# Moving the opening loads of a hybrid decoder block: half a weight tile, the gate weights and the other constants

## The chip, the cores and the metric

The kernel runs on one core of a Trainium2 chip. The metric is the time of one execution in device microseconds (us). A core has five engines with an instruction queue each: TensorE (PE, matmuls; its weight loads are listed apart as PEld), VectorE (DVE), ScalarE (ACT), GpSimd (POOL) and SyncE (SP, which only issues DMAs). ScalarE and GpSimd can issue DMAs too; a DMA stands in the queue of the engine that issues it, and all queues are served by the core's 16 DMA engines. An engine works through its instructions in the order in which they were written for it: an instruction that waits holds up all that stand behind it.

## The reference

One decoder layer for 2048 tokens of width 1024, in float32. The input is normalised and projected once into the columns of two branches, which are mixed, gated, joined, projected out and added to the input; a last norm follows.

```python
n = rms_norm(h, norm_w[layer])
proj = jnp.einsum('bsd,de->bse', n, w_in[layer])
pu, pz, q, k, v, dz, b, a = [proj[..., int(offsets[i]):int(offsets[i + 1])] ...]
y_pool = pool_mixer(pu, pz, pool_w[layer], pool_scale[layer])
y_dn = deltanet_mixer(q, k, v, dz, b, a, conv_w[layer], a_log[layer], dt_bias[layer], dn_norm_w[layer])
y = jnp.concatenate([y_pool, y_dn], axis=-1)
h = h + jnp.einsum('bse,ed->bsd', y, w_out[layer])
...
return rms_norm(h, final_norm_w)
```

`pu` and `pz` (512 columns each) feed a causal pooling mixer with trailing windows of 2, 4, 8 and 16 tokens, `q`, `k`, `v`, `dz` (4 heads of 128 each) a gated delta rule in chunks with a short causal convolution, and `b`, `a` (4 columns each) are its gates, which the text calls the gate columns.

## The kernel before

**Tiling.** The tokens are taken in two blocks of 1024, each in two halves of 512. For the projection, tokens stand along the free axis: x is read transposed (`xT`), a tile of 128 input features by 512 tokens is one matmul step, and eight such steps (k = 0 to 7) sum one output tile of 128 columns in PSUM. Float32 is carried as two parts of the type float32r: a high part and the rest. `split_x` (L522) makes `nh` (ScalarE, L525) and `nl` (VectorE, L526) from an x tile, `split_w` (L713) makes `wh` (ScalarE, L716) and `wl` (VectorE, L717, recorded as L510) from a weight tile, and `project` (L722) issues three matmuls a step: `wh` with `nh` (L728), `wh` with `nl` (L729), `wl` with `nh` (L730). The norm's factor for each token is not applied to x; it is worked out from the rows of x beside the projection, and multiplied in when the sums are taken from PSUM.

**The opening.** The order of the first loads is as follows.

- ScalarE issues `norm_w`, both halves of the first weight tile (256 KB each, tile `qT`, L706) and the first constants `cst` (L1112).
- SyncE issues x of the first half in five pieces (L520; the first tile in two pieces, then tiles of two steps and 512 KB: two in tiles named `dec`, one `kdec`), the two halves of the second weight tile (L706), x of the second half (four tiles: `dec`, `kdec`, `kT`, `kT`), four row tiles of the first half (L533: `Ai`, `At`, `v`, `vT`, 512 KB each) and four of the second (`Tt`, `Tt`, `yr1`, `Ai`).
- `load_constants` (L475) then adds the gate weights `wba` (32 KB), two triangular matrices (`tri`, a tile named `X`, 128 KB), `dt_bias`, `a_log` (`nega`), the convolution's weights, `pool_w` (256 KB), `pool_scale` and the head norm's weight, all on SyncE.
- GpSimd issues the third weight tile (`wh`, 512 KB) at the start and adds its rest later (L720).

**What uses them.** Of each row tile ScalarE takes the sum of squares (L539); when the four of a half are done, `row_scale` (L541, GpSimd's L507), `row_diagonal` (L547, four VectorE scalings, L550) and a matmul against ones (`broadcast`, L554; L556) spread the norm's factors over the partitions (`rb`), and only then can that half's sums be taken from PSUM. The gate weights are split like the others: `whl` by a cast on ScalarE (L495) and a subtraction on VectorE (L496), both in `prepare_constants` (L494). The gate columns are a projection of their own (`gate_rows`, L560).

**What sets the order.** The program is traced as a list of events, each with a slot (`at`, L674). A `Planner` (L91) then writes the order of every engine anew: it knows a modelled cost for each instruction (L126), goes through modelled time, and lets each engine take the ready instruction that is due first, unless that would hold up one that is due sooner and ready soon (L306 to L321). Due times are worked backwards from PE's sequence in event order (L238 to L254). PE takes runs of matmuls in event order as far as they are ready, looking up to 24 runs ahead (L287). The DMAs traced before the mark `plan.opening` (L476) are taken in their traced order on their engine (L255, L308 to L314), and their landing is modelled as one pipe that all of them share (L387 to L389); other DMAs get a landing time of their own (L133 to L139). The planned order is bound (L396), so at run time nothing overtakes. A DMA of SyncE or ScalarE beyond the first eight also waits for an older one to land.

**Slots of the events concerned.** First weight tile -80, `cst` -79.5, x of the first half -79 to -76, second weight tile -72, x of the second half -71 to -68, rows -67 and -62, `load_constants` (and with it the opening mark) -45, `prepare_constants` -1.

Of the kernel before, what the change touches and what calls it, by code (L numbers as in the profile page):

```python
# [17 lines left out]
KT = D // P  # L18
# [41 lines left out]
E_PU, E_PZ, E_Q, E_K, E_V, E_Z = 0, 4, 8, 12, 16, 20  # L60
# [344 lines left out]
def hymba_kernel(  # L405
# [19 lines left out]
    nc = tc.nc  # L425
# [9 lines left out]
    plan = Planner(tc, nc.cur_bb.bb.instructions)  # L435

    def st(shape, dt, tag, bufs=1):
        return plan.tile(sp, shape, dt, tag, tag, bufs)


    def ct(shape, dt, name):
        return cp.tile(shape, dt, tag=name, name=name)
# [10 lines left out]
    wba = ct([P, KT, 8], F32, "wba")  # L453
# [19 lines left out]
            nc.tensor.matmul(ps[:, 0:P], ones, ones, start=True, stop=True)  # L473

    def load_constants():  # L475
        plan.opening = len(plan.traced)  # L476
        tri = st([P, 2, P], F32, "X")
        for dst, src in (
            (wba, w_ba),
            (tri, consts[:, C_LE:C_X0].rearrange("p (a b) -> p a b", a=2)),  # L480
            (dtb, dt_bias[None, :].to_broadcast([P, HEADS])),
            (nega, a_log[None, :].to_broadcast([P, HEADS])),
            (cw, conv_w),
            (pw, pool_w),
            (psc, pool_scale),
            (dnw, dn_w),
        ):
            nc.sync.dma_start(dst, src)
        nc.gpsimd.memset(halo_c, 0.0)
        nc.gpsimd.memset(halo_p, 0.0)  # L490
        nc.gpsimd.memset(state, 0.0)
        return tri
# [181 lines left out]
    def at(slot, fn, *args):  # L674
        events.append((slot, len(events), fn, args))
# [22 lines left out]
    def load_w(w, et, first):  # L698
        w["hi"] = st([P, KT, P], F32R, "wh", 3)
        w["lo"] = st([P, KT, P], F32R, "wl", 3)  # L700
        if first:
            w["raw"] = wr = st([P, KT, P], F32, *first)
            step = KT // 2
            eng = nc.scalar if et == E_PU else nc.sync
            for k in range(0, KT, step):
                eng.dma_start(wr[:, k : k + step], w_in[et, :, k : k + step])  # L706
        elif w["mixed"]:
            nc.gpsimd.dma_start(w["hi"], mixed[et - E_PU, 0])
            nc.gpsimd.dma_start(w["lo"], mixed[et - E_PU, 1])
        else:  # L710
            nc.gpsimd.dma_start(w["hi"], w_in[et])  # L711

    def split_w(w, et, first, part):  # L713
        if first:
            ks = slice(part * KT // 2, (part + 1) * KT // 2)
            nc.scalar.copy(w["hi"][:, ks], w["raw"][:, ks])  # L716
            split_lo(nc.vector, w["lo"][:, ks], w["raw"][:, ks], w["hi"][:, ks])  # L717
        elif not w["mixed"]:
            nc.scalar.activation(w["lo"], w["hi"].bitcast(F32), AF.Copy, scale=-1.0)  # L719
            nc.gpsimd.dma_start(w["lo"], w_in[et], accum_op=ALU.add)  # L720
# [31 lines left out]
    def gate(u, dst, rb):  # L752
        nc.vector.tensor_tensor(out=dst, in0=u["ps"], in1=rb, op=ALU.mult)
        nc.scalar.activation(dst, dst, AF.Silu)
# [355 lines left out]
    tri = []  # L1110
    at(-90, begin)
    at(-79.5, lambda: nc.scalar.dma_start(cst, consts[:, 0:C_TMP]))  # L1112
    at(-89, warm_up)
    at(-45, lambda: tri.append(load_constants()))
    at(-1, lambda: prepare_constants(tri[0]))
    for b in range(NB):
        n, gt = [None, None], {}
        units = []
        heads = [(h, {}) for h in range(HEADS)]
        pools = [(gi, {}) for gi in range(GROUPS)]  # L1120
        tiles = []
        for gi, res in pools[:lead]:
            tiles += [("pu", E_PU + gi, gi, res), ("pz", E_PZ + gi, gi, res)]
        for h, res in heads:
            kinds = (("k", E_K), ("q", E_Q), ("v", E_V), ("z", E_Z))
            tiles += [(kind, e0 + h, h, res) for kind, e0 in kinds]
        for gi, res in pools[lead:]:
            tiles += [("pu", E_PU + gi, gi, res), ("pz", E_PZ + gi, gi, res)]
        order = []
        i = 0  # L1130
        while i < len(tiles):
            if tiles[i][0] == "pu":
                order += [(tiles[i], 0), (tiles[i + 1], 0), (tiles[i], 1), (tiles[i + 1], 1)]
                i += 2
            else:
                order += [(tiles[i], 0), (tiles[i], 1)]
                i += 1
        for hf in range(NHALF):
            n[hf] = env = {}
            base = slot - (1 - hf) * 8 * PAIRED + 0.5  # L1140
            for i in range(KT // 2):
                at(base - L_X if b else -79 + 8 * hf + i, load_x, b, hf, i, env)
            for k in range(KT):
                at(base + 0.1 + k * (8 * PAIRED - 2) / KT, split_x, k, env)
            base += 8 * PAIRED - 2
            base += L_ROW if b else L_ROW0[hf]
            for j in range(NCH):
                at(base - L_XT + 4 * j if b else -67 + 5 * hf + 0.1 * j, load_rows, b, hf, j, env)
                at(base - L_XT + 8 + 4 * j if b else 4 + 8 * hf + j, square_rows, j, env)
            at(base - L_XT + 24 if b else base, row_scale, env)  # L1150
            at(base, row_diagonal, env)
            at(base + L_RB[b * NHALF + hf], broadcast, env)
            env["slot"] = base + L_RB[b * NHALF + hf] + 0.1
        for hf in range(NHALF):
            tg = slot + 8 * PAIRED * hf + (L_GR if b else L_GR0)
            at(tg, gate_rows, n, hf, gt)
            at(tg + L_GROW, gate_scale, n, hf, gt)
            at(tg + L_GROW + L_GCOL, gate_turn, hf, gt)
        ready = tg + L_GROW + L_GCOL + 0.1
        at(ready, gate_columns, gt)  # L1160
        ready += L_GATE
        at(ready, gate_sums, gt)
        ready += L_SUMS
        for h in range(HEADS):
            for hf in range(NHALF):
                at(ready + L_DEC * (2 * h + hf), decay, gt, h, hf)
        ready += L_DEC + 2
        ends = [dict() for _ in range(HEADS)]
        weights = {}
        for (kind, et, idx, res), hf in order:  # L1170
            if et not in weights:
                weights[et] = {"mixed": kind == "pu" and idx >= lead}
                first = ("qT", 2) if slot < 8 * PAIRED else None
                at(-80 + slot if first else slot - L_W, load_w, weights[et], et, first)
                at(slot - (16 if first else L_SPLIT), split_w, weights[et], et, first, 0)
                if first:
                    at(slot - 13, split_w, weights[et], et, first, 1)
            u = {"spare": 24 <= slot < 40}
            for k in range(KT):
                at(slot + k, lambda u=u, w=weights[et], n=n, hf=hf, k=k: project(u, w, n, hf, k))  # L1180
            slot += KT
            te = max(slot, n[hf]["slot"])
            if kind in "kqv":
                key = kind + "T"

                def evac(u=u, kind=kind, idx=idx, hf=hf, res=res, key=key, env=n[hf]):
                    if hf == 0:
                        res[key] = st([P, TB], F32, key, 1 if kind == "v" else 2)
                    conv_silu(u, "qkv".index(kind) * HEADS + idx, hf, res[key], env["rb"])

            elif kind == "z":

                def evac(u=u, hf=hf, res=res, env=n[hf]):
                    if hf == 0:
                        res["sz"] = st([P, TB], F32, "sz", 2)
                    gate(u, res["sz"][:, hf * HALF : (hf + 1) * HALF], env["rb"])

            elif kind == "pz":

                def evac(u=u, hf=hf, res=res, env=n[hf]):  # L1200
                    res["szp"] = st([P, HALF], F32, "szp", 1)
                    gate(u, res["szp"], env["rb"])

            else:

                def evac(u=u, b=b, idx=idx, hf=hf, env=n[hf]):
                    pool_mix(u, b, idx, hf, env["rb"])

                at(te + L_POOL, pool_out, u, b, idx, hf, res, weights[et]["mixed"])
            at(te, evac)  # L1210
            if kind in "kqvz":
                ends[idx][kind, hf] = slot
        for h, res in heads:
            delta(b, h, res, gt, ends[h], ready)
# [229 lines left out]
    for k in range(NP):  # L1444
        w = {}
# [110 lines left out]
```

## Time and profile before

| | |
|---|---|
| three runs | 934.34, 934.75, 937.35 us; median 934.75 |
| profiled execution | 933.28 us, of which the core's span 931.6 us |
| granted clock of TensorE, mean of the span | 0.991 |
| busy: PE, DVE, ACT, POOL | 909.4, 606.9, 475.1, 171.6 us |
| DMA | 124.20 MB, mean 133 GB/s |

How to read it: the profile is of one execution. "Busy" counts instructions that work; waits and the issuing of DMAs don't count. In a row of the timeline stand the start, the duration, the engine (a small q marks its sequencer, which issues DMAs), the line, the operation, the tiles written and read, the number of instructions, and in brackets how long the engine sat idle before it and what released it. A row of waits has who waited for whom, the sum in us, how often, and the longest. A row of DMA issues has the tiles, the issuing engine, how many, the size of one, and the median time from issue to landing. Tile names come without their number, so that several tiles share one (`dec`, `kT`, `qT`). The kernel's loads and casts of the opening take place in the first 60 us.

### The profile page before, as it was taken

To read this page: it belongs to the slowest core of one execution; us is meant where nothing else is said; L and a number is where in the kernel's file an instruction comes from. 1 tells how busy PE (TensorE), PEld (TensorE's weight loads), DVE (VectorE), ACT (ScalarE), POOL (GpSimd) and SP (SyncE) were. 2 spreads that over 40 slices of the span, in tenths; PEclk is the share of its full clock that TensorE was granted. 3 is DMA by queue.
4 is the path that set the end of the run, shared out by engine and by line. 5 is a ranking of instruction groups with operands and counts; after the bars stand their busy time and mean duration, and the time that the engine had idled before them with its cause. 6 is when DMAs were issued, how large, how long until landed. Compare 5 with 4: busy or idle time off the path is not lost.

```text
span 931.6 us, 14634 instructions
## 1 busy us (share of the span) xinstructions
PE 909.4 (98%) x5194; PEld 738.5 (79%) x5194; DVE 606.9 (65%) x1621; ACT 475.1 (51%) x1227; POOL 171.6 (18%) x212
## 2 busy tenths in 40 slices
PE   8799999999999999999999999999999999999996
PEld 6578878887888878867888887888887888888885
DVE  5376965864856845756685576775763487976563
ACT  6539654456455445443945545545533445444442
POOL 1216210111211110202711120121011101022221
PEclk9899999999999999999999999999999999999998
DMA  9643574353353485733345244353247486476644
GB/s 353 192 98 80 146 170 98 59 125 74 61 139 96 100 264 164 196 86 90 80 104 125 63 88 111 74 108 91 55 111 247 133 265 208 134 184 162 162 112 125
DMA packets 84569, 124.20 MB, mean 133 GB/s; under 512 B 32144, under 2 KB 49808, under 8 KB 84496
## 3 DMA queue, kind: packets, MB, share of 16 engines
q0 software_dynamic: 17280, 56.89, 28.4%
q1 hardware_dynamic: 66640, 65.75, 22.4%
q8 instruction: 41, 0.67, 0.3%
q10 hardware_dynamic: 576, 0.63, 0.2%
q14 instruction: 32, 0.26, 0.1%
HBM read 101.22 MB, written 22.02 MB: 132 GB/s over the span
## 4 chain that ended last, share of the span: by engine, by line
PE 83%; DMA 5%; DVE 5%; ACT 3%; issue 2%; SPq 1%; POOL 0%; POOLq 0%; DVEq 0%; ACTq 0%
PE ps L728 16%; PE ps L730 16%; PE ps L729 16%; PE psA L1410 2%; PE ch L1018 2%; PE psA L1411 2%; PE psA L1409 2%; PE tp L820 2%; PE ch L1012 2%; PE ch L996 2%; PE pso L1297 2%; PE pso L1295 2%; PE pso L1296 2%; PE ob L1022 1%; PE ob L1006 1%
## 5 line engine op out<-in xcount | busy, mean ns | idle before, releaser
L728 PE MATMUL ps<-nh,wh 128*128 128x512 f32 x768 | 326.3, 425 | 7.4 <-ACT nh L525 7.4
L730 PE MATMUL ps<-nh,wl 128*128 128x512 f32 x768 | 302.0, 393 | 0.0
L729 PE MATMUL ps<-nl,wh 128*128 128x512 f32 x768 | 301.6, 393 | 0.0
L728 PEld LDWEIGHTS ps<-nh,wh 128*128 128x128 f32 x768 | 145.7, 190 | 33.4 <-ACT nh L525 8.3
L730 PEld LDWEIGHTS ps<-nh,wl 128*128 128x128 f32 x768 | 144.8, 189 | 31.9 <-DVE wl L510 0.2
L729 PEld LDWEIGHTS ps<-nl,wh 128*128 128x128 f32 x768 | 145.9, 190 | 24.0 <-issue 1.7
L742 DVE SCALAR_TENSOR_TENSOR acc<-u,cw,acc 128x512 f32<-128x512 f32 x144 | 113.6, 789 | 19.0 <-ACT acc L740 16.8
L711 POOL DMA_DIRECT2D wh<-in_w_in_dram x40 | 23.3, 583 | 305.8 <-PE ps L730 294.9
L719 ACT ACTIVATE wl<-wh 128x1024 fp32r<-128x1024 f32 x40 | 42.3, 1059 | 54.4 <-DMA wh<-in_w_in_dram 46.8
L720 POOL DMA_DIRECT2D wl<-in_w_in_dram x40 | 35.1, 877 | 174.0 <-ACT wl L719 140.2
L737 DVE TENSOR_TENSOR u<-ps,rb 128x512 f32<-128x512 f32 x48 | 33.1, 689 | 43.9 <-PE ps L730 43.7
L899 DVE TENSOR_TENSOR tmp<-Ai,X 128x60 f32<-128x60 f32 (+24 forms) x248 | 54.1, 218 | 7.6 <-DMA Ai<-blocks 1.1
L905 DVE TENSOR_TENSOR X<-X,tmp 128x60 f32<-128x60 f32 (+24 forms) x248 | 53.8, 217 | 6.9
L740 ACT ACTIVATE acc<-u,cw 128x512 f32<-128x512 f32 x48 | 34.8, 724 | 39.2 <-DVE u L737 38.5
L1025 ACT ACTIVATE sqj<-v 128x128 f32<-128x128 f32 x64 | 19.8, 309 | 67.4 <-DVE v L1023 62.1
L1019 DVE SCALAR_TENSOR_TENSOR state<-state,ex,ch 128x128 f32<-128x128 f32 x64 | 22.0, 344 | 33.7 <-PE ch L1018 33.3
L827 ACT ACTIVATE sqj<-tp 128x128 f32<-128x128 f32 x128 | 33.6, 277 | 4.9 <-PE tp L820 4.7
L1014 ACT ACTIVATE nv<-ch,sm 128x128 f32<-128x128 f32 x64 | 23.5, 367 | 23.1 <-PE ch L1012 22.9
L1417 POOL DMA_DIRECT2D dec<-in_x_dram x23 | 19.9, 865 | 77.0 <-ACT dec L1416 76.9
L1008 ACT ACTIVATE o<-ob,ex 128x128 f32<-128x128 f32 x64 | 23.6, 369 | 18.0 <-PE ob L1006 17.8
L1018 PEld LDWEIGHTS ch<-nv,kdec 128*128 128x128 f32 x128 | 20.1, 189 | 11.8 <-ACT nv L1014 10.6
L1304 ACT ACTIVATE t<-dec 128x512 f32<-128x512 f32 x32 | 20.2, 632 | 17.3 <-DVE dec L1302 16.8
(292 smaller groups left out, 1719.9 us busy)
## 6 DMA issues: line engine op xcount, KB each, us to landing
wh<-in_w_in_dram POOLq DMA_DIRECT2D x40, 512.0 KB, 3.8
wl<-in_w_in_dram POOLq DMA_DIRECT2D x40, 512.0 KB, 5.7
y_dram<-yt SPq DMA_DIRECT2D x32, 256.0 KB, 4.2
out_dram<-dec SPq DMA_DIRECT2D x14, 512.0 KB, 4.4
dec<-in_x_dram POOLq DMA_DIRECT2D x23, 256.0 KB, 4.1
yr<-in_x_dram SPq DMA_DIRECT2D x9, 512.0 KB, 4.5
Ai<-blocks SPq DMA_DIRECT2D x32, 128.0 KB, 2.7
yr<-y_dram SPq DMA_DIRECT2D x8, 512.0 KB, 4.4
```

What stands on the lines that cost most here:

```text
L719: nc.scalar.activation(w["lo"], w["hi"].bitcast(F32), AF.Copy, scale=-1.0)
L720: nc.gpsimd.dma_start(w["lo"], w_in[et], accum_op=ALU.add)
L728: nc.tensor.matmul(ps, w["hi"][:, k], nh[:, k], start=(k == 0), stop=False)
L729: nc.tensor.matmul(ps, w["hi"][:, k], nl[:, k], start=False, stop=False)
L730: nc.tensor.matmul(ps, w["lo"][:, k], nh[:, k], start=False, stop=(k == KT - 1))
L737: nc.vector.tensor_tensor(out=ub[:, HALO:], in0=ps, in1=rb, op=ALU.mult)
L740: nc.scalar.activation(acc, ub[:, HALO:], AF.Copy, scale=cw[:, ci, CONV - 1 : CONV])
L742: nc.vector.scalar_tensor_tensor(out=acc, in0=ub[:, h0 + j : h0 + j + HALF], scalar=cw[:, ci, j : j + 1], in1=acc, op0=ALU.mult, op1=ALU.add,)
L827: nc.scalar.activation(junk, tp[:, j], AF.Square, accum_out=dst[:, c : c + 1])
L899: nc.vector.tensor_tensor(out=tmp[:, 0:n, 0:w], in0=Ai[:, j, j + 1 : BS].unsqueeze(1).to_broadcast([P, n, w]), in1=X[:, 0:n, j : j + 1].to ...
L905: nc.vector.tensor_tensor(out=X[:, 0:n, j + 1 : BS], in0=X[:, 0:n, j + 1 : BS], in1=tmp[:, 0:n, 0:w], op=ALU.subtract)
L1018: nc.tensor.matmul(ch[:, 2], e["kdec"][:, c], nv, start=True, stop=True)
```

## The change

Three edits. The second half of the first weight tile is no longer issued by ScalarE behind the first half, but by SyncE, behind x of steps 0 to 3 and ahead of x of steps 4 to 7 (`load_w_rest` at slot -77.5). The gate weights are issued by ScalarE behind `cst` (slot -79.4). `load_constants`, now with seven DMAs, moves from slot -45 to -64.5, between the rows of the first half and those of the second, still on SyncE. The opening mark is set by an event of its own at slot -58, behind the last rows, so that all these DMAs belong to the opening.

```diff
     def load_constants():
-        plan.opening = len(plan.traced)
         tri = st([P, 2, P], F32, "X")
         for dst, src in (
-            (wba, w_ba),
             (tri, consts[:, C_LE:C_X0].rearrange("p (a b) -> p a b", a=2)),
...
             step = KT // 2
-            eng = nc.scalar if et == E_PU else nc.sync
-            for k in range(0, KT, step):
+            for k in range(0, KT if et != E_PU else step, step):
+                eng = nc.scalar if et == E_PU else nc.sync
                 eng.dma_start(wr[:, k : k + step], w_in[et, :, k : k + step])
...
+    def load_w_rest(w, et):
+        nc.sync.dma_start(w["raw"][:, KT // 2 :], w_in[et, :, KT // 2 :])
...
     at(-79.5, lambda: nc.scalar.dma_start(cst, consts[:, 0:C_TMP]))
+    at(-79.4, lambda: nc.scalar.dma_start(wba, w_ba))
     at(-89, warm_up)
-    at(-45, lambda: tri.append(load_constants()))
+    at(-64.5, lambda: tri.append(load_constants()))
+    at(-58, lambda: setattr(plan, "opening", len(plan.traced)))
...
                 at(slot - (16 if first else L_SPLIT), split_w, weights[et], et, first, 0)
+                if et == E_PU and first:
+                    at(-77.5, load_w_rest, weights[et], et)
```

## The prediction

> **What bounds the kernel now.** I read the page first. TensorE (PE) is busy for 98% of the span, so there is little idle time to win, and all of it is countable.
>
> ```profile
> span 931.6 us, 14634 instructions
> PE 909.4 (98%) x5194; PEld 738.5 (79%) x5194; DVE 606.9 (65%) x1621; ACT 475.1 (51%) x1227; POOL 171.6 (18%) x212
> ```
>
> The view of waits, kept to PE, says where the idle time is.
>
> ```profile
> PE ps L728 <- ACT nh L525: 7.4, 2, 5.0
> PE tp L820 <- ACT kT L750: 2.0, 1, 2.0
> ```
>
> Two waits of the projection's matmuls for the high parts of x (`nh`, L525) hold 7.4 us; the next largest, in the stage of the heads, holds 2.0. The timeline puts both into the opening: PE's last matmul before the first wait starts at 7.67, and the second wait runs from 28.83 (28.44 + 0.39) to 33.83.
>
> ```profile
> 7.67 0.39 PE L730 MATMUL ps<-nh,wl 128*128 128x512 f32 x1
> 10.47 0.79 PE L728 MATMUL ps<-nh,wh 128*128 128x512 f32 x1 [2.41 <-ACT nh L525]
> 28.44 0.39 PE L730 MATMUL ps<-nh,wl 128*128 128x512 f32 x1
> 33.83 0.79 PE L728 MATMUL ps<-nh,wh 128*128 128x512 f32 x1 [4.99 <-ACT nh L525]
> 46.59 1.12 PE L556 MATMUL psr<-sacc,ones 128*128 128x512 f32 x2
> ```
>
> ScalarE's timeline says why `nh` is late each time.
>
> ```profile
> 9.00 0.62 ACT L716 CAST wh<-qT 128x512 fp32r<-128x512 f32 x1 [2.53 <-DMA qT<-in_w_in_dram]
> 9.69 2.77 ACT L525 ACTIVATE nh<-dec,nw 128x512 fp32r<-128x512 f32 x4
> ...
> 22.78 0.19 ACT L539 ACTIVATION_READ_ACCUMULATOR At<-At 128x1 f32 x1
> 30.83 0.24 ACT L495 CAST whl<-wba 128x64 fp32r<-128x64 f32 x1 [7.86 <-DMA wba<-in_w_ba_dram]
> 30.98 1.05 ACT L539 ACTIVATE v<-v 128x1024 f32<-128x1024 f32 x1
> ...
> 33.07 1.32 ACT L525 ACTIVATE nh<-kT,nw 128x512 fp32r<-128x512 f32 x2
> 34.29 1.05 ACT L539 ACTIVATE Tt<-Tt 128x1024 f32<-128x1024 f32 x1
> ```
>
> Second wait: the cast of the gate weights (L495) stands in ScalarE's order ahead of two row squares (30.98 to 33.07) and the last two `nh`, and sits 7.86 us until `wba` lands. First wait: the cast of the first weight tile's second half (L716) is ahead of the third `nh` and waits until 9.00. The DMA issues, each with its time to landing, show that this is only half of the reason.
>
> ```profile
> 1.71 0.43 SPq L520 DMA_DIRECT2D dec<-in_xT_dram  x1
> dec<-in_xT_dram SPq DMA_DIRECT2D x1, 512.0 KB, 8.0
> qT<-in_w_in_dram ACTq DMA_DIRECT2D x1, 256.0 KB, 7.2
> 13.84 0.33 SPq L533 DMA_DIRECT2D vT<-in_x_dram  x1
> vT<-in_x_dram SPq DMA_DIRECT2D x1, 512.0 KB, 11.6
> 19.26 0.33 SPq L488 DMA_DIRECT2D wba<-in_w_ba_dram  x1
> wba<-in_w_ba_dram SPq DMA_DIRECT2D x1, 32.0 KB, 11.5
> ```
>
> The second x tile (matmul steps 2 and 3), issued at 1.71, lands 8.0 later, at about 9.7. So the third `nh` at 9.69 starts as its own data lands; the weight half is not the last thing it waits for. `wba` took 11.5 us for 32 KB because it was issued at 19.26 behind the rows.
>
> The windows view, cut where the clock changes, gives the stretch and its length, the busy time of each engine with the number of its records, the granted clock (PEclk), the DMA share and GB/s.
>
> ```profile
> core 0: us, PE busy (x) PEld busy (x) DVE busy (x) ACT busy (x) POOL busy (x), PEclk, DMA share, GB/s
> 6.99:10.41 3.42, 1.06 (x5) 0.46 (x3) 0.96 (x2) 1.33 (x3) 0.00 (x0) 1.00 1.06 401
> 10.41:13.82 3.41, 3.35 (x7) 2.39 (x8) 3.35 (x5) 3.27 (x7) 0.00 (x0) 0.50 1.05 386
> 33.83:37.71 3.88, 3.88 (x7) 2.45 (x8) 2.23 (x6) 3.67 (x7) 2.56 (x3) 0.50 0.00 0
> ```
>
> After each gap PE works at a granted clock of 0.50: for 3.35 us after the first, 3.88 after the second. The second gap thus costs 4.99 and another 3.88 / 2 = 1.94.
>
> **The change part by part.**
>
> *Second half of the weight tile to SyncE.* ScalarE issues one weight DMA fewer and SyncE one more, behind two x tiles and ahead of the last two. From 4 to 8 us three queues share the engines:
>
> ```profile
> q1 hardware_dynamic: 291, 0.55, 38.4%
> q0 software_dynamic: 142, 0.52, 35.5%
> q10 hardware_dynamic: 305, 0.47, 32.1%
> ```
>
> q1 is SyncE's, q10 ScalarE's, q0 GpSimd's (the third tile's weights). SyncE's x gets little over a third while ScalarE's halves run beside it. Without the 256 KB on q10 the second x tile lands sooner by at most 262 KB / 386 GB/s = 0.68 us, by nothing if it is paced elsewhere; constants and gate weights stay on q10 and q0 has its share, so I take two thirds, 0.45: 9.22 instead of 9.67. The third `nh` then starts at 9.25 and PE at 10.02. The half itself, now behind that tile, lands about 9.22 + 0.68 = 9.9, later than the 9.00 of before; it is due at matmul step 4, six matmuls after 10.02. In the half-clock window PE has x7 in 3.35 us, so six take up to 2.9 and the step comes by 12.9; behind the third and fourth `nh` (2.77 / 4 = 0.69 each) the cast runs from 10.6 to 11.3, and it fits. If the order written for ScalarE keeps this cast ahead of the third `nh`, that starts at 10.55 and PE at 11.3: a loss of 0.85. So this term is a gain of 0.45, ends -0.85 and +0.68.
>
> [...]
>
> SyncE's issue costs about 0.46 (four in 1.84, below). One landing slot goes too: after the first eight DMAs an issue waits for an old one to land.
>
> ```profile
> 0.81 1.84 SPq L520 DMA_DIRECT2D dec<-in_xT_dram  x4
> 3.97 0.37 SPq L520 DMA_DIRECT2D kdec<-in_xT_dram  x1
> ```
>
> With the half and the gate weights among the first eight it is the third x tile, issued now at 2.2, that takes its place at 3.97. The engines carry 386 GB/s and more through those windows with what is queued ahead of it, so this is covered; uncovered it would be 1.8 us.
>
> *Gate weights on ScalarE's queue.* 32 KB at 386 GB/s are 0.08 us for everything behind. Landed by about 7, the cast (0.24) and its VectorE half go into ScalarE's and VectorE's idle gaps before 9 us. Then nothing holds ScalarE at 22.97 (end of the second square): the third row comes before the fourth, and the fourth lands at 13.84 + 11.6 = 25.46 (+0.08), its square and sum end at 26.6, and the two `nh` start at 26.6 and 27.3. PE, 0.45 earlier, needs them at 28.4. Covered with 1 us to spare. So the second gap goes whole: 4.99, and with it the half clock, 1.94. Ends: 0.7 (under B below) and 4.99; for the clock 0 and 1.94.
>
> *Other constants ahead of the second half's rows.* Seven DMAs, some 414 KB by the sizes of their tiles, now go between the fourth and the fifth row. Their price is in the landings at the end of the load phase:
>
> ```profile
> 15.19 1.68 SPq L533 DMA_DIRECT2D Tt<-in_x_dram  x2
> Tt<-in_x_dram SPq DMA_DIRECT2D x1, 512.0 KB, 12.8
> 21.71 0.33 SPq L533 DMA_DIRECT2D Ai<-in_x_dram  x1
> Ai<-in_x_dram SPq DMA_DIRECT2D x1, 512.0 KB, 10.4
> 30.63 0.33 SPq L488 DMA_DIRECT2D nega<-in_a_log_dram  x1
> nega<-in_a_log_dram SPq DMA_DIRECT2D x1, 2.0 KB, 3.0
> ```
>
> The last row landed at 32.1, the last of the six constants behind it at 33.6: 1.5 us. So the four late rows land 1.5 later, the last at 33.6. Their issues move more: eight DMAs after the fourth row, the fifth's issue waits for that row at 25.5 instead of 15.2. What is then queued is only the constants, and 3.0 us is the landing of a small DMA, so the fifth row comes at 28.5 to 29.5 (28.0 now): same answer. What is late next: ScalarE squares the last row at 33.6 to 34.8, the row sums, GpSimd's rsqrt and four VectorE scalings follow (the last two take 1.06 and 0.88 in the rows below), so the second broadcast (L556, 46.59 now) can run at 37.1.
>
> ```profile
> 41.71 1.06 POOL L507 TENSOR_TENSOR rstd<-ms,mhalf 128x4 f32<-128x4 f32 x1
> 42.80 0.88 DVE L550 TENSOR_SCALAR sacc<-cst,rstd 128x128 f32<-128x128 f32 x4 [0.78 <-POOL rstd L507]
> ```
>
> PE reaches it at 46.59 - 7.4 = 39.2: covered by 2.1 us, so it costs nothing; with that cover gone, at most the 1.5.
>
> **The sum.** 0.45 + 4.99 + 1.94 = 7.4 us. After 38 us only PE sets the pace, and its work there starts from the projections and gates that move with it, so I let the whole sum reach the end. The profiled execution took 933.28 us (span 931.6 and 1.7 around it): 925.9. The runs' median is 934.75, 1.5 above it: 927.3.
>
> **The rivals.**
>
> *A, the forecast:* both gaps as above, 927.3; with the bounds of its first term 927.1 to 928.6.
>
> *B, the second gap gets a new cause.* ScalarE's order is written anew by the planner, and one or two squares of the later rows come ahead of the last two `nh`. The fifth row lands at 29.5 by the working above; one square in front lets PE go on at 31.4, two (30.8 + 1.05 + 0.75) at 32.6. A gap of 3.0 to 4.2 stays, with its half clock: gain 0.45 + 2.0 or 0.8, so 932.3 to 933.5. For it: those squares are due early in the plan. Against: they come behind the `nh` now (34.29 after 33.07), and their data is later by the change.
>
> *C, the first gap no longer costs clock.* In 6.99 to 10.41 PE was busy 1.06 of 3.42 us and 0.50 followed. PE back at 10.02 makes it 1.45 of 3.42; if that is enough, 3.35 / 2 = 1.7 us more are won: 925.6. No row shows a limit between 1.06 and 3.35. [...]
>
> *D, slower: the order made anew costs more downstream than the opening gives.* The planner orders every engine's whole program from modelled times, and the change alters these from the first DMA on. Its place would be the heads' stage, where one wait of 2.0 us (L820 for L750) stands now; there are eight heads. If each of the seven others got such a wait, 14 us are lost: 934.75 - 7.4 + 14 = 941.4. It decides from the fourth such wait on (8 against 7.4). Against it: the modelled times move by tenths of a microsecond, and due times come from PE's fixed sequence.
>
> *E, the change does not do what it says:* the opening's DMAs are taken in the order traced, so the moves are made; I give this nothing apart from B.
>
> **How the numbers follow.** A 0.66, C 0.10, B 0.14, D 0.10. A difference under 0.3% (2.8 us) cannot be told from none here: the bound is 931.95. A and C are faster (0.76), B is within it (0.14), D slower (0.10). The prediction is A's 927.3. The range, 924 to 933, reaches from 1.6 below C, for an order that falls out a little better downstream (as far as 8 tenths of the one wait of 2.0 there), over A to most of B, and leaves out D.
>
> **What would show it.** Right: the cast L495 before 10 us without a long wait, no PE gap at 28, PE at full clock from 14 us on, the first gap near 2 us. Step by step: the second x tile landing near 9.2, the weight half near 9.9, the fourth row still near 25.5, the fifth at 28.5 to 29.5, the second broadcast without an idle PE before it. Wrong: ScalarE waiting for a row or for `tri` ahead of the last `nh`; a PE gap at the first or second broadcast; new PE waits in the heads' stage that add up to several us.

## The result, and the profile after

The changed kernel takes 928.13 us (median of 4 runs, 927.5 to 929.41) against 935.31 of the kernel before (4 runs beside it, 934.34 to 937.35): a ratio of 0.9928, 95% interval 0.9915 to 0.9940. That is 0.72% faster, 7.2 us; 927.3 and a gain of 7.4 had been forecast. The profiled execution took 928.51 us, 4.77 less than the one before, at a mean granted clock of 0.995.

The page's head and the first rows of the waits of PE, after:

```profile
span 926.8 us, 14634 instructions
PE 909.3 (98%) x5194; PEld 736.9 (80%) x5194; DVE 606.5 (65%) x1621; ACT 475.5 (51%) x1227; POOL 172.0 (19%) x212
PE tp L821 <- ACT kT L751: 2.1, 1, 2.1
PE ps L729 <- ACT nh L523: 1.1, 1, 1.1
PE tp L574 <- DVE ba L567: 0.9, 2, 0.7
```

The work is the same to a few tenths of a microsecond. The two waits for `nh` (7.4 us before) have become one of 1.1, the wait of the heads' stage is as it was, and a small new one stands beside them: the gate columns' transposes (`tp`, L574) wait for VectorE's `ba`.

PE's timeline after, at the places of the two gaps, of the new wait and of the heads' stage:

```profile
9.35 0.49 PE L729 MATMUL ps<-nh,wh 128*128 128x512 f32 x1 [1.06 <-ACT nh L523]
28.00 0.40 PE L729 MATMUL ps<-nh,wh 128*128 128x512 f32 x1
37.95 0.42 PE L574 MATMUL tp<-cst,ba 16*128 16x16 f32 x4 [0.69 <-DVE ba L567]
114.42 0.66 PE L821 MATMUL tp<-cst,kT 128*128 128x128 f32 x4 [2.06 <-ACT kT L751]
```

The first gap is 1.06 instead of 2.41 us, and at 28.00 PE works on where it stood for 4.99.

ScalarE's timeline after:

```profile
8.57 1.33 ACT L523 ACTIVATE nh<-dec,nw 128x512 fp32r<-128x512 f32 x2 [1.86 <-DMA dec<-in_xT_dram]
9.81 0.60 ACT L717 CAST wh<-qT 128x512 fp32r<-128x512 f32 x1
10.32 0.24 ACT L493 CAST whl<-wba 128x64 fp32r<-128x64 f32 x1
...
24.83 1.06 ACT L537 ACTIVATE vT<-vT 128x1024 f32<-128x1024 f32 x1 [0.97 <-DMA vT<-in_x_dram]
25.89 1.32 ACT L523 ACTIVATE nh<-kT,nw 128x512 fp32r<-128x512 f32 x2
27.84 0.20 ACT L498 ACTIVATE nega<-nega 128x4 f32<-128x4 f32 x1 [0.63 <-DMA nega<-in_a_log_dram]
30.66 0.56 ACT L556 COPY rb<-psr 128x512 f32<-128x512 f32 x1
...
34.15 1.28 ACT L755 ACT_TABLE_LOAD   x1
35.44 0.63 ACT L755 ACTIVATE szp<-szp 128x512 f32<-128x512 f32 x1
35.98 1.04 ACT L537 ACTIVATE Ai<-Ai 128x1024 f32<-128x1024 f32 x1
43.06 0.59 ACT L556 COPY rb<-psr 128x512 f32<-128x512 f32 x1 [5.00 <-PE psr L554]
```

The order is the one that the prediction built: `nh` of the second x tile at 8.57, then the weight half (9.81), then the gate weights' cast (10.32, no wait; forecast before 10, with `wba` landing by about 7, where it landed at 9.5), and the last `nh` at 25.89 as the fourth row's square ends. Two places matter below. `nega` at 27.84 waits only 0.63 us for `a_log`, and the last row's square (35.98) runs behind a table load and `szp`, although its data landed at 34.2. VectorE's timeline shows who waits for that square:

```profile
37.14 0.17 DVE L541 TENSOR_SCALAR ms<-ms 128x4 f32<-128x4 f32 x1 [2.52 <-ACT Ai L537]
37.22 0.67 DVE L567 TENSOR_TENSOR ba<-psba,rb 16x512 f32<-16x512 f32 x1
```

`ms`, the sums of squares of the second half, waits 2.52 us for it, and `ba`, which PE needs, stands behind `ms`.

The DMA issues after, each with its time to landing; by the timeline they were issued at 1.71, 2.18, 24.83 and 28.42:

```profile
dec<-in_xT_dram SPq DMA_DIRECT2D x1, 512.0 KB, 6.8
qT<-in_w_in_dram SPq DMA_DIRECT2D x1, 256.0 KB, 7.2
Tt<-in_x_dram SPq DMA_DIRECT2D x1, 512.0 KB, 4.8
Ai<-in_x_dram SPq DMA_DIRECT2D x1, 512.0 KB, 5.8
```

So the second x tile landed at 8.5 (forecast 9.2), the weight half at 9.4 (9.9), the fifth row at 29.6 (28.5 to 29.5), the last row at 34.2 (33.6).

The windows view, cut into stretches of 3.41 us, on whose bounds every change of the granted clock in these two profiles lies (before at 10.41, 13.82, 30.89, 37.71 and 925.18, after at 115.50, 118.91 and 921.04), first the kernel before, then the one after:

```profile
27.47:30.89 3.42, 1.36 (x7) 0.78 (x5) 0.00 (x0) 0.06 (x1) 0.00 (x0) 1.00 1.03 406
119.63:123.04 3.41, 1.58 (x9) 1.41 (x10) 1.77 (x3) 1.99 (x9) 0.00 (x0) 1.00 0.75 154
123.04:126.45 3.41, 3.41 (x21) 2.94 (x20) 2.41 (x7) 2.59 (x8) 0.55 (x1) 1.00 0.80 232
```

```profile
6.27:9.68 3.41, 2.35 (x7) 0.99 (x7) 1.58 (x3) 1.55 (x3) 0.00 (x0) 1.00 1.08 392
9.68:13.10 3.42, 2.84 (x10) 1.62 (x10) 3.39 (x7) 3.21 (x7) 0.00 (x0) 1.00 1.05 389
112.08:115.50 3.42, 1.36 (x10) 1.09 (x9) 2.18 (x4) 1.49 (x5) 0.00 (x0) 1.00 0.63 114
115.50:118.91 3.41, 3.41 (x10) 2.62 (x9) 1.47 (x7) 2.50 (x11) 0.55 (x1) 0.50 0.63 183
```

Before, three windows at half clock lay in the opening (10.41 to 13.82 and 30.89 to 37.71) and none at the wait of the heads' stage. After, the opening has none, and the same 2.06 us of the heads' stage are followed by one.

Where the 4.8 us of the two profiles come from is read from the start of the n-th matmul in the one and in the other. PE's lead over the kernel before is 1.49 us at the 40th matmul, 6.63 at the 101st (the second gap is gone), 8.6 at the 108th (its half clock too), 7.03 from about 52 us on, 5.47 behind the half-clock window at 115.5, and 4.8 from 380 us to the end. Of the fall from 8.6 to 7.03 three small waits between 32 and 51 us make 1.1 (0.22, 0.69 and 0.23); the other 0.4 is not resolved. PE's order differs from that of before only within the 118th to the 184th of its 5194 matmuls.

### The profile page after: what moved, and what is told of

It is laid out like the page before. It is cut to its first block, busy times and chain, and to the rows that moved or that the text cites. A ratio compares the mean times of both kernels' runs of the same rounds, so it can differ in the third digit from the quotient of the medians.

```text
span 926.8 us, 14634 instructions
## 1 busy us (share of the span) xinstructions
PE 909.3 (98%) x5194; PEld 736.9 (80%) x5194; DVE 606.5 (65%) x1621; ACT 475.5 (51%) x1227; POOL 172.0 (19%) x212
## 4 chain that ended last, share of the span: by engine, by line
PE 76%; DVE 7%; issue 6%; DMA 6%; ACT 3%; POOL 1%; SPq 1%; POOLq 0%; DVEq 0%; ACTq 0%
PE ps L729 14%; PE ps L731 14%; PE ps L730 14%; PE psA L1415 2%; PE psA L1416 2%; PE psA L1414 2%; DVE tmp L900 2%; DVE X L906 2%; PE tp L821 2%; PE pso L1302 2%; PE pso L1301 2%; PE pso L1300 2%; PE ch L1019 2%; PE ch L1013 1%; PE ch L997 1%
## 5 line engine op out<-in xcount | busy, mean ns | idle before, releaser
L1020 DVE SCALAR_TENSOR_TENSOR state<-state,ex,ch 128x128 f32<-128x128 f32 x64 | 22.0, 344 | 34.2 <-PE ch L1019 34.0
L828 ACT ACTIVATE sqj<-tp 128x128 f32<-128x128 f32 x128 | 33.6, 277 | 4.6 <-PE tp L821 4.5
L999 DVE SCALAR_TENSOR_TENSOR rho<-ch,negc,v 128x128 f32<-128x128 f32 x64 | 22.2, 347 | 10.4 <-PE ch L997 9.0
```

The source lines that it names most:

```text
L828: nc.scalar.activation(junk, tp[:, j], AF.Square, accum_out=dst[:, c : c + 1])
```

## The experiments

All times are medians with the ratio to runs of the kernel before on the same chip. In the first four, each part of the change stands alone, or two stand without the third.

**The gate weights alone** (e1), on ScalarE's queue; the half and the other constants as before.

```diff
-            (wba, w_ba),
...
+    at(-79.4, lambda: nc.scalar.dma_start(wba, w_ba))
```

> Only the gate weights move (ScalarE's queue, behind cst); the weight half stays on ScalarE, the seven constants stay where they were. Theory G (the second gap is the gate weights' late landing, and nothing else): PE's first gap stays near 2.4 us, the gap at 28.8 is gone with its half clock, gain 6.5 to 7 us. Theory N (with the gap gone ScalarE runs into the next late constant): in its planned order the Exp of a_log (nega) now stands behind the two first squares of the later rows and ahead of the copy of the first broadcast (rb); a_log lands at about 33.6, the last of the constants, so rb comes at 34 instead of 30.7, and PE waits 2 to 3 us at the gate columns near 33 us, perhaps with a half-clock window: gain 3 to 5 us.

Measured: 930.63 us, ratio 0.9949 (0.9931 to 0.9967), 4 us faster and not 7. The second gap is gone, but another stands behind it, from 32.4 to 35.2 us, by ScalarE's and PE's timeline:

```profile
30.54 0.19 ACT L538 ACTIVATION_READ_ACCUMULATOR Tt<-Tt 128x1 f32 x1
33.69 0.21 ACT L499 ACTIVATE nega<-nega 128x4 f32<-128x4 f32 x1 [2.96 <-DMA nega<-in_a_log_dram]
33.80 0.57 ACT L557 COPY rb<-psr 128x512 f32<-128x512 f32 x1
...
35.15 0.61 PE L563 MATMUL psba<-nh,whl 128*16 128x512 f32 x1 [2.72 <-DVE u L765]
```

ScalarE now stops 2.96 us at the exponential of `a_log`, 2 KB that SyncE issued at 29.57 behind the rows. Behind it in ScalarE's order is the copy of the broadcast (`rb`), without which VectorE can't take the first sums from PSUM, and PE stops 2.72 us for a free PSUM tile. The half clock follows here too, from 35.04 to 38.46.

In the kernel before this landing cost nothing, since there the exponential stood behind the copy. ScalarE's timeline of the kernel before:

```profile
38.37 0.59 ACT L558 COPY rb<-psr 128x512 f32<-128x512 f32 x1 [0.87 <-PE psr L556]
...
39.91 0.20 ACT L500 ACTIVATE nega<-nega 128x4 f32<-128x4 f32 x1
```

`a_log` had landed at 33.6 (30.63 and 3.0), long before 39.91. In e1 and e4 the order that the planner wrote has the exponential ahead of the copy, and so `a_log` is the next late load in the way.

**The weight half alone** (e2), on SyncE; the gate weights and constants as before.

```diff
-            eng = nc.scalar if et == E_PU else nc.sync
-            for k in range(0, KT, step):
+            for k in range(0, KT if et != E_PU else step, step):
+                eng = nc.scalar if et == E_PU else nc.sync
...
+                    at(-77.5, load_w_rest, weights[et], et)
```

> Only the second half of the first weight tile moves to SyncE. Theory S (the prediction's first term): the second x tile lands 0.5 to 1.1 us sooner than the 9.67 of before, the first gap is 1 to 2 us instead of 2.4, and the second gap of 5 us with its half clock stays: gain 0.5 to 1.3 us, and up to 1.7 more if the clock window after the first gap stays at full rate. Rival: the sooner landing in the changed kernel came from a late start of GpSimd's weight transfer alone; then the tile lands at 9.4 to 9.7 here and the gain is 0 to 0.3.

Measured: 935.62 us, ratio 1.0008 (0.9997 to 1.0018). Alone it is worth nothing, as the rival forecast, and the second x tile landed at 9.41. The rival's reason does not hold, though: GpSimd's transfer is issued at 1.42 or 1.43 in this profile as in those of the kernel before and of the changed kernel. By ScalarE's and PE's timeline the second gap stands as before:

```profile
31.77 0.25 ACT L495 CAST whl<-wba 128x64 fp32r<-128x64 f32 x1 [8.47 <-DMA wba<-in_w_ba_dram]
...
34.77 0.80 PE L731 MATMUL ps<-nh,wh 128*128 128x512 f32 x1 [6.67 <-ACT nh L525]
```

What PE may win at the first gap it waits for at the second, which ends when `wba` lands (in this profile at 31.75, 0.9 later than before). So this run says what the edit is worth in the kernel before, and not what it is worth beside the other two. f1 asks that.

**The other constants alone** (e3): `load_constants`, with `wba` as its first DMA, at slot -64.5, still all on SyncE; neither the half nor the gate weights change their queue.

```diff
-        plan.opening = len(plan.traced)
...
-    at(-45, lambda: tri.append(load_constants()))
+    at(-64.5, lambda: tri.append(load_constants()))
+    at(-58, lambda: setattr(plan, "opening", len(plan.traced)))
```

> Only load_constants moves ahead of the later rows, with the gate weights as its first DMA, all on SyncE; the weight half stays on ScalarE. Theory O (order, not the queue, closes the second gap): the gate weights land at 25.5 to 27.5 behind the fourth row, ScalarE casts them behind the fourth square, the last two nh start before 28, and PE's gap at 28.8 is 0 to 0.5 us: gain 6 to 7 us, as much as the gate weights at once would give. Theory G (only the gate weights at once closes it): the gap shrinks to 1 to 3 us and keeps its half clock, gain 2 to 4 us.

Measured: 927.49 us, ratio 0.9917 (0.9895 to 0.9938): the whole gain, with one edit of the three. ScalarE's timeline:

```profile
26.97 0.24 ACT L494 CAST whl<-wba 128x64 fp32r<-128x64 f32 x1 [1.47 <-DMA wba<-in_w_ba_dram]
27.12 1.33 ACT L524 ACTIVATE nh<-kT,nw 128x512 fp32r<-128x512 f32 x2
28.36 0.19 ACT L499 ACTIVATE nega<-nega 128x4 f32<-128x4 f32 x1
29.76 0.59 ACT L557 COPY rb<-psr 128x512 f32<-128x512 f32 x1 [0.82 <-PE psr L555]
```

The cast still waits for `wba`, but only 1.47 us, since it is issued right behind the fourth row (14.38), and not behind the seventh (19.26 before). The two `nh` follow at 27.12, soon enough: between 11.1 and 113 us PE has no wait above 0.3. `nega` doesn't wait at all. So the gate weights had only to come before the second half's rows, not on another queue.

**The half and the gate weights, the constants left** (e4): the changed kernel without its third edit.

```diff
+        plan.opening = len(plan.traced)
...
-    at(-64.5, lambda: tri.append(load_constants()))
-    at(-58, lambda: setattr(plan, "opening", len(plan.traced)))
+    at(-45, lambda: tri.append(load_constants()))
```

> The changed kernel without its third edit: weight half on SyncE, gate weights on ScalarE, the seven constants back at their old place behind the rows. By the prediction (the third edit is covered, or costs at most 1.5 us) this is as fast as the changed kernel or up to 1.5 us faster: gain 7 to 8.5 us. By theory N (the third edit earns its place because a_log is next to be late) PE waits 2 to 3 us near 33 us for the copy of the first broadcast behind the Exp of a_log: gain 4 to 5.5 us.

Measured: 930.24 us, ratio 0.9944 (0.9926 to 0.9963), with the same stop as e1, by ScalarE's timeline:

```profile
33.81 0.21 ACT L499 ACTIVATE nega<-nega 128x4 f32<-128x4 f32 x1 [3.02 <-DMA nega<-in_a_log_dram]
```

In this profile PE loses 1.55 us to it, where e1 lost 2.72. The medians of e4 and of the changed kernel differ by 2.1 us (930.24 and 928.13), by their ratios 1.5; those of e1 and e3, run side by side, by 3.1, but these two also differ in the gate weights' queue. The intervals of either pair touch, so the size is loose; that there is a stop, and who waits for it, is what the traces show.

**The change without the half's move** (f1): the gate weights and the constants, both weight halves on ScalarE.

```diff
-            for k in range(0, KT if et != E_PU else step, step):
-                eng = nc.scalar if et == E_PU else nc.sync
+            eng = nc.scalar if et == E_PU else nc.sync
+            for k in range(0, KT, step):
...
-                    at(-77.5, load_w_rest, weights[et], et)
```

> The changed kernel without its first edit: the weight half stays on ScalarE behind the first half; gate weights on ScalarE and constants ahead as in the change. Theory W (moving the half is worth its 0.45 us or more): 0.5 to 1 us slower than the changed kernel beside it, first gap 2 to 2.4 us. Theory 0 (the half alone gave nothing against the kernel before, and the landing of the second x tile scatters by about a microsecond from run to run whichever queue carries the half): the same as the changed kernel within 1 us, gain 6 to 7.5 us, first gap anywhere from 1.5 to 2.4 us.

Measured: 930.24 us (927.51 to 932.01), ratio 0.9950 (0.9934 to 0.9965). Neither theory fits well: it is 1.3 us slower than the changed kernel beside it (f3), more than W's 0.5 to 1, with a first gap of 1.15 us, less than either gave. In its profile the second x tile landed late, at 10.4, and PE waited 0.9 us for the cast of the first weight half ahead of that and 1.3 for `ba` behind it. Whether the missing edit is the reason can't be read from one such run; the table further down takes it up.

**`a_log` alone** (f2): e4, with `a_log` on ScalarE's queue behind the gate weights and the other constants left at slot -45.

```diff
-            (nega, a_log[None, :].to_broadcast([P, HEADS])),
...
+    at(-79.3, lambda: nc.scalar.dma_start(nega, a_log[None, :].to_broadcast([P, HEADS])))
```

> The kernel with weight half and gate weights moved and the constants at their old place, and in addition a_log alone issued by ScalarE at the start. Theory N (what the third edit is worth is a_log, for which ScalarE waited 3.02 us ahead of the first broadcast's copy): that wait and PE's gap of 1.55 us near 35 us are gone with the half clock they may bring; gain 6.5 to 8 us, about the changed kernel. Rival (another of the late constants, pool_w or the triangular matrices, is next to hold an engine): a gap of 1 to 3 us stays between 32 and 40 us, gain 4 to 5.5 us.

Measured: 928.67 us, ratio 0.9931 (0.9918 to 0.9945). ScalarE's timeline has no wait ahead of `rb` any more:

```profile
32.04 0.19 ACT L537 ACTIVATION_READ_ACCUMULATOR Tt<-Tt 128x1 f32 x1
32.14 0.56 ACT L556 COPY rb<-psr 128x512 f32<-128x512 f32 x1
```

With `a_log` alone in time the stop is gone and the time is that of the changed kernel within the intervals, 6 us less than before (forecast 6.5 to 8). So of the constants that the third edit moves, these 2 KB are what ScalarE stopped for. The time itself is not clear of e4's: 0.9931 and 0.9944, with intervals that overlap.

**The changed kernel again** (f3), unaltered, and **the constants alone again** (f4), run side by side.

```diff
(f3: nothing against the changed kernel; f4: nothing against e3)
```

> The changed kernel unaltered, on this chip, for comparison with the others: gain 6.5 to 7.5 us as on record. In the profile the opening has the same gaps (first gap 1 to 2 us, none at 28) but clock windows lie elsewhere: if the half-clock stretch after the 2 us gap of the heads' stage is a matter of where the free-running window falls, it need not come back; if it belongs to this kernel, it does.

> load_constants alone ahead of the later rows, gate weights first in it, on SyncE, once more and beside the changed kernel. In the first look PE led the kernel before by 8.5 us after 50 us (the changed kernel: 7.0), as the second broadcast's copy came at 39.3 instead of 43.1. If that is the order's doing, it is faster than the changed kernel by 0.5 to 1.5 us; if the lead was a fast draw of the loads, the two are equal within 0.5.

Measured: 928.9 us for f3, ratio 0.9940 (0.9927 to 0.9953), and 928.18 for f4, ratio 0.9926 (0.9913 to 0.9939). The intervals overlap as they do in the first runs (0.9915 to 0.9940 and 0.9895 to 0.9938): one edit alone does as well as the three, and the 0.5 to 1.5 us by which it might be faster are not shown. What the profiles repeat is where the order matters: from the 120th to the 200th matmul PE's lead falls by 1.2 us in the changed kernel (8.2 to 7.0) and in f3 (8.1 to 6.9), by at most 0.1 in e3 (8.56 to 8.47) and f4 (6.97 to 6.92). f3 also has the half clock in the heads' stage again, from 115.37 us. f4 shows where a lead is lost later. By its timelines of ScalarE and PE:

```profile
157.43 1.06 ACT L718 ACTIVATE wl<-wh 128x1024 fp32r<-128x1024 f32 x1 [3.97 <-DMA wh<-in_w_in_dram]
...
159.34 0.49 PE L1017 MATMUL ch<-nv,kdec 128*128 128x128 f32 x2 [1.67 <-ACT nv L1013]
```

ScalarE stops 3.97 us for a weight tile's load, and PE, being ahead, waits for the small work behind. This is a place where part of a lead is spent; here it took 1.67 us.

**GpSimd's tile later, in the changed kernel** (g1): four clears of the third weight tile before its own load, so that its 512 KB enter the queue some 4 us later (the four took 4.01 us in its profile). The question is what paces the second x tile, if not the weight half.

```diff
+            for _ in range(4 if w["late"] else 0):
+                nc.gpsimd.memset(w["hi"].bitcast(F32), 0.0)
             nc.gpsimd.dma_start(w["hi"], w_in[et])
...
+                weights[et] = {"mixed": kind == "pu" and idx >= lead, "late": b == 0 and et == E_K}
```

> The changed kernel with GpSimd's load of the third weight tile held back by four fills of that tile (about 1 us each), so that its transfer starts near 8 us instead of 4.3. Theory P (what paces the second x tile is the sharing with GpSimd's 512 KB, not the queue of the weight half): the second x tile lands at 7.5 to 8.2 instead of 8.6 to 9.5 and the first gap is under 1 us; whether the end is earlier depends on the next wait (the first broadcast's copy at 30.7), gain against the changed kernel 0 to 1.5 us. Rival (the landing is paced by the issue and the latency of SyncE's DMAs): it lands at 8.6 or later, gap 1.1 to 2 us, no gain. Either way the third tile's rest comes later, which may hold PE near 31 us by up to 3 us; then it is slower than the changed kernel.

**The same, with the constants alone** (g2): the edit of g1 put on e3, whose weight half is on ScalarE's queue.

> The same hold of the third weight tile in the kernel with load_constants alone moved (both halves of the first tile on ScalarE). Theory P: the second x tile lands at 7.7 to 8.6 instead of 8.6 to 9.8, as the weight half still shares with it, some 0.5 us later than with the half on SyncE; first gap 0.5 to 1.5 us. If the queue of the half mattered beside GpSimd's share, it shows here, where that share is gone: the tile lands 0.4 to 0.7 us later than in the run beside it. Gain against the kernel before 6.5 to 8.5 us.

Measured: 931.69 us for g1, ratio 0.9962 (0.9948 to 0.9976), and 929.05 for g2, ratio 0.9930 (0.9912 to 0.9948). The DMA issues, of g1 and of g2, both issued at 1.71:

```profile
dec<-in_xT_dram SPq DMA_DIRECT2D x1, 512.0 KB, 6.1
```

```profile
dec<-in_xT_dram SPq DMA_DIRECT2D x1, 512.0 KB, 6.0
```

The second x tile lands at 7.8 and 7.7, sooner than in any of the ten other profiles (8.55 to 10.38) and with the weight half on either queue. So it is GpSimd's tile whose share of the engines holds it back. The time is not won, though: in g1 the cast of the weight tile after it, itself later by then, waits 4.16 us on ScalarE with the last row's square behind it, and PE waits 2.84 for `ba`; in g2 PE waits 1.70 for the rest of a weight tile and 1.17 for `ba`. By PE's timeline of g1:

```profile
40.20 0.42 PE L574 MATMUL tp<-cst,ba 16*128 16x16 f32 x4 [2.84 <-DVE ba L567]
```

**What the profiles say together of the first edit.** The landing of the second x tile, and PE's lead over the kernel before at the 80th matmul, which stands behind the first gap and ahead of the second:

| weight half on | kernels | x tile lands, us | mean | lead at the 80th matmul, us | mean |
|---|---|---|---|---|---|
| ScalarE | before, e1, e3, f1, f4 | 9.67, 9.13, 8.59, 10.38, 9.83 | 9.52 | 0, 1.47, 1.32, 0.20, -0.27 | 0.54 |
| SyncE | after, e2, e4, f2, f3 | 8.55, 9.41, 8.87, 9.51, 9.18 | 9.10 | 1.47, 0.72, 0.10, -0.75, 0.92 | 0.49 |

The tile lands 0.42 us sooner on the mean, but single landings scatter over 1 to 1.8 us, and the lead is the same. Of the times, f1 against the changed kernel speaks for the edit (0.9950 against 0.9928 and 0.9940), e4 against e1 says nothing (0.9944 and 0.9949), and e3 and f4, with the half on ScalarE (0.9917 and 0.9926), speak against it; all these intervals overlap. That it is worth anything isn't shown, nor that it costs anything.

## Why the prediction was right, and where it was not

**The second gap: right, in cause and size.** The gate weights' landing held ScalarE's order. With them there in time the gap is gone, whether they come on ScalarE's queue (e1, e4, after) or early on SyncE's (e3, f4). The prediction gave 4.99 us and 1.94 for the clock, 6.93; PE's lead grows from 1.47 at the 100th to 8.6 at the 108th matmul, 7.1. Rival B, a new cause in the same place, did not come: in every profile of e1 to f4 with the gate weights early the fourth row's square is directly followed by the last `nh`, or by them behind the short cast. The row squares named by B stand behind.

**The third edit: a stop that was not foreseen.** "Other constants ahead of the second half's rows" was to cost nothing, and at most 1.5. The traces show what it takes away: without it (e1, e4) ScalarE stops 3 us for `a_log` ahead of the first broadcast's copy, and PE 2.72 and 1.55; in the changed kernel ScalarE waits 0.63 for it, and with `a_log` alone in time (f2) not at all. The step that failed is "what is late next": it followed the four late rows to the second broadcast, and did not ask which other instructions that wait for a DMA could hold ScalarE. The issue of `a_log` at 30.63 and its landing 3.0 later were quoted in that same part. In the order of before its exponential stood behind the copy; rival B said that ScalarE's order is written anew, but thought of row squares alone.

What the edit is worth in time is loose: 3.1 us between e1 and e3 (not the one edit alone), 1.5 between e4 and the changed kernel by their ratios, 0.4 between e4 and the changed kernel run again (f3), nothing between e1 and f1 (0.9949 and 0.9950). One reason for so little stands in the next paragraph: the changed kernel loses 1.2 us at the second broadcast, which f2 (6.46 to 6.41 there) does not. Whether an order with the copy ahead of the exponential would do as well without moving `a_log` was not run. With the constants left, the prediction's reasoning would have forecast 927.3, and e4 measured 930.24: the two edits that it credited do not give the sum by themselves.

**The cover of the second broadcast: used up, not kept.** It was to be run at 37.1 with 2.1 us to spare. The last row landed at 34.2, 0.6 later than forecast, but its square started at 35.98, 1.8 after that, since ScalarE first took a table load and `szp`; VectorE's `ms` and `ba` stood behind it, PE's second broadcast came at 42.01 and the copy at 43.06. PE filled most of that time with other matmuls and lost 1.1 us in small waits. In e3 the planner left all squares ahead of the table load; the last ran at 34.59, the copy came at 39.26, and PE's lead is 8.5 us at that point; f4 repeats it. With the late rows at nearly the same place (34.5 in e3) the loss is absent, so it is mostly the written order's and not the landing's.

**The first gap: the mechanism stands in part, the price does not.** Without the half on ScalarE's queue the tile was to land 0.45 sooner. The mean over five profiles each is 0.42, but this is well inside their scatter, and PE's mean lead behind the gap is 0.54 without the edit and 0.49 with it. GpSimd's 512 KB hold the tile by more (7.7 and 7.8 against a mean of 9.1 and 9.5). So the runs do not tell the term's 0.45 from its other end, nothing "if it is paced elsewhere".

**The clock, rival C: it happened in the profiled run, but not with its numbers.** C asked whether 1.45 us of work in 3.42 suffice, and said that no row shows a limit between 1.06 and 3.35. The profile of before had two such rows, shown above: 1.36 was followed by half clock, 1.58 was not. After, the gap was 1.06 us long and left 2.35 and 2.84 us of work in its window and the next, and full clock followed. 1.45 itself would hardly have sufficed: in the heads' stage of f1 it was followed by 0.50. It also counts where a gap falls in the windows of 3.41 us. Before, the changes at 10.41 and 30.89 are six of them apart (20.48). Between two profiles of one kernel their place differs: bounds lie at 5.92 and 9.33 us in e3 (the change at 917.28 is 266 windows behind 9.33), at 7.36 and 10.77 in f4. In e3 the first gap was 2.17 us long, nearly as before, but split between two windows, and full clock followed; its windows view:

```profile
5.92:9.33 3.41, 2.19 (x8) 0.89 (x6) 1.38 (x2) 0.96 (x2) 0.00 (x0) 1.00 1.07 396
9.33:12.75 3.42, 2.18 (x8) 1.55 (x9) 3.12 (x5) 3.42 (x7) 0.00 (x0) 1.00 1.05 391
12.75:16.16 3.41, 3.41 (x16) 2.79 (x16) 3.41 (x7) 3.34 (x6) 0.00 (x0) 1.00 1.05 387
```

The changed kernel has a half-clock window in the heads' stage instead, where its gap of 2.06 us lay in one window and left 1.36 of work: 1.56 us of lead went there (7.03 to 5.47). f3, the same kernel again, has the same window at half clock. Of the twelve profiles four have it (after, f3, f1 and e4); before, at 119.63, the same gap cost nothing beyond itself.

**The sum: close, in part by luck.** The profiled run gained 4.8 and not 7.4: 8.6 by the 108th matmul, 1.2 more than forecast (1.0 of it at the first gap), less 1.6 around the second broadcast, 1.6 in the heads' stage and 0.7 behind it. Of these losses the forecast named the first alone, as a bound of 1.5 that it did not expect. "I let the whole sum reach the end" thus failed in the profiles. The runs' medians differ by more, 7.2, since the execution profiled before lies 2.0 under its median and the one after 0.4 above. Of the other runs only the mean clock is known, 0.995 in most of f3's and 0.990 to 0.993 in those of the kernel before, so that remainder stays open.

**Rival D, a worse order downstream: did not come.** PE's order is as before but for the opening, and the wait of the heads' stage stayed one of 2.06 us, not eight. Its cause shows in small at the second broadcast, where the order made anew costs some 1.2 us.

## What to carry to other kernels

Before a wait is taken away, go down that engine's order behind it, write down for each instruction fed by a DMA when that lands, and price the change to the next one that is late: here that was 2 KB, for which ScalarE stopped 3 us. Where a planner writes the order anew, do this with the order of the changed kernel; in that of before, the late load stood where it did no harm. Order the loads by first use rather than by size, and try each edit alone: one line moved had all the gain of the three. In the opening, where the engines moved 347 to 396 GB/s, a transfer came sooner when another was held back in time (7.7 and 7.8 us against 8.55 to 10.38); handing its neighbour to another queue showed no gain (PE's mean lead was 0.54 us without and 0.49 with it).

## What the runs showed of the hardware

**After how much work in a window half clock followed.** Over the twelve profiles' openings and heads' stages, each of the nine full-clock windows in which PE was busy at most 1.45 us of 3.41 (from 0.00 in e2 to 1.45 in f1) was followed by one at 0.50, and none with more than 2.16 us. Between lie both: 1.74 (e4, below), 1.91 (f2), 1.87 (g1) and 2.16 (g2) were followed by half clock, 1.56 (e2), 1.58 (before, the row at 119.63 above) and others up to 2.14 (g2) were not. The windows view of e4:

```profile
8.21:11.63 3.42, 1.74 (x7) 1.01 (x6) 1.98 (x4) 2.68 (x6) 0.00 (x0) 1.00 1.05 394
11.63:15.04 3.41, 3.40 (x9) 2.33 (x8) 3.41 (x8) 3.04 (x7) 0.00 (x0) 0.50 1.06 389
```

So PE's busy time alone doesn't decide there, and what else does stays open.

**The same gap had two prices.** The wait of the heads' stage, 2.03 to 2.07 us in all profiles but g2's (1.39), was followed by half clock in four of the twelve, which cost 1.56 us more in the one where the lead was followed through it (after). By an estimate from these rows (windows of 3.41 us, with 1.36 us of work left beside the gap after and 1.58 before), moving a program by one or two microseconds can gain or lose that much at a gap that the change doesn't touch.

**Landings scatter in a full queue.** In the first 10 us the same 512 KB on the same queue landed between 8.55 and 10.38 us in the ten profiles of the table, and in two profiles of one kernel at 8.55 and 9.18 (after, f3) or 8.59 and 9.83 (e3, f4). What the 16 engines moved from 4 to 8 us differs too: 389 to 396 GB/s in the four profiles that landed by 9.13, 347 to 386 in the other six; why is open. A gain of 0.45 us there can't be read from one pair of profiles; it needs several, or the times.
